# The last matrix product of a hybrid attention layer, formed by seven half products per pair of row tiles

## The chip, the cores and the metric

The kernel runs on one core of one Trainium2 chip, in one launch. The metric is device time in microseconds (us). A run takes the time of the whole execution; the span below is the part that the hardware profiler shows of the one profiled execution.

## The reference

The kernel computes a decoder layer with two attention mixers. Only its end matters here. `y_a` and `y_b` are the mixers' projections, `m_a` and `m_b` slices of an earlier projection, S = D = 1024, and all is float32.

```python
mod = c @ w_ada[l] + b_ada[l]
shift, scale, gate = jnp.split(mod, 3, axis=-1)
...
y = (jax.nn.sigmoid(m_a) * y_a + jax.nn.sigmoid(m_b) * y_b) @ w_out[l]
x = x + gate[:, None, :] * rms_norm(y, g_post[l])
```

`rms_norm(y, g)` is `y * rsqrt(mean(y*y) + eps) * g` along each row.

## The kernel before

A float32 matrix is held as two fp32r halves, high and low: ScalarE casts the high one, and a subtraction on VectorE or POOL makes the low one. A product is then three matmuls of 128x128 weights with 128x512 columns: high by high, high by low, low by high. The tile scheduler orders the instructions of each engine, waits follow from tiles and their pools (a tag with `bufs` buffers), and `chain` and `after` add an order without a wait. Products go to the eight PSUM banks in a fixed turn (`anybank`, L114).

The work around the change has three stages.

The gated stage (L954 to L1003) forms the merged `y`, transposed, in eight blocks of 128 channels, `ym`. `gated(m, "B", 1, ...)` takes for each block two halves of 512 tokens, 12 matmuls each (L956 to L958), gates from DRAM with a sigmoid on ScalarE, and one multiplication on VectorE (L985). After every second block `heads_out` loads two halves of a head pair and splits them (cast L925, subtraction L926), and for each block `w_out_block` loads 128 rows of `w_out` in two halves, casts them (L978) and subtracts on POOL (L979). `gated(m, "A", 0, ...)` then multiplies (L992) and adds (L993) for the same blocks, and the block is split: cast on ScalarE, subtraction L1003 on VectorE.

The gate sums (L1005 to L1014) make the last third of `mod`: eight loads of 512 KB into `wa`, eight VectorE instructions over 128x1024 (L1011), each with a short row that reads its sum out. `gate_rows` (L1017 to L1026) spreads `mod` times `g_post` over all partitions: a VectorE multiplication makes the operand (L1022), TensorE multiplies by ones (L1025), ScalarE copies the two halves to `ggb`.

The last product (L1063 to L1068) has eight row tiles of 128 tokens. `out_products` (L1028) makes both halves of a tile, 24 matmuls each (L1034 to L1036). `out_rows` (L1040) squares both on ScalarE (L1049), multiplies the first by its gate (L1052), makes the mean (L1053, L1055), takes the power on POOL (L1056), multiplies the second half (L1057), multiplies by the power and adds `x` (L1060), and stores (L1061). Two tiles are ahead; the gate rows stand behind them:

```python
ahead = [out_products(0), out_products(1)]
gate_rows()
for i in range(NT):
    out_rows(i, ahead.pop(0))
    if i + 2 < NT:
        ahead.append(out_products(i + 2))
```

Of the kernel before, what the change touches and what calls it, by code (L numbers as in the profile page):

```python
# [7 lines left out]
F32 = mybir.dt.float32  # L8
# [6 lines left out]
P = 128  # L15
# [52 lines left out]
def hybrid_kernel(tc, io, out):  # L68
# [843 lines left out]
    with tc.tile_pool(name="ot", bufs=1, reuse_waits="tile") as op:  # L912
        oh = [op.tile([P, S], F32R, name=f"oh{k}", tag=f"oh{k}") for k in range(8)]
        ol = [op.tile([P, S], F32R, name=f"ol{k}", tag=f"ol{k}") for k in range(8)]
        ym = {}
# [4 lines left out]
        def heads_out(k):  # L920
            for half in range(2):
# [19 lines left out]
        for n, name in enumerate(MERGE[:KEEP]):  # L941
            sg = op.tile([P, S], F32, name="sgm", tag=f"ym{7 - n}")
# [23 lines left out]
        woh, wol = [], []  # L966
        ymh, yml = [], []

        def w_out_block(k):

            a, b = [], []
            for n in range(2):
                ns = slice(n * HS, n * HS + HS)
                raw = wp.tile([P, HS], F32, name="wraw", tag="wraw", bufs=3)
                nc.sync.dma_start(raw, io["w_out"][k * P : (k + 1) * P, ns])
                a.append(main.tile([P, HS], F32R, name=f"woh{k}", tag=f"hh{k}_{n}"))
                b.append(main.tile([P, HS], F32R, name=f"wol{k}", tag=f"hl{k}_{n}"))
                nc.scalar.copy(a[n], raw)  # L978
                nc.gpsimd.tensor_tensor(b[n], raw, a[n].bitcast(F32), ALU.subtract)  # L979
            woh.append(a)  # L980
            wol.append(b)

        for m in range(8):
            ym[m] = op.tile([P, S], F32, name=f"ym{m}", tag=f"ym{m}")
            gated(m, "B", 1, lambda sl, ty, sg: nc.vector.tensor_tensor(ym[m][:, sl], ty, sg, ALU.mult))  # L985
            if m % 2:
                heads_out(m // 2)
            w_out_block(m)
        for m in range(8):

            def emit(sl, ty, sg):
                nc.vector.tensor_tensor(sg, ty, sg, ALU.mult)  # L992
                nc.vector.tensor_tensor(ym[m][:, sl], ym[m][:, sl], sg, ALU.add)  # L993
# [4 lines left out]
            ymh.append(op.tile([P, S], F32R, name=f"ymh{m}", tag=places[m][0]))  # L998
            yml.append(op.tile([P, S], F32R, name=f"yml{m}", tag=places[m][1]))
            for half in range(2):  # L1000
                sl = slice(half * HS, half * HS + HS)
                nc.scalar.copy(ymh[m][:, sl], ym[m][:, sl])
                nc.vector.tensor_tensor(yml[m][:, sl], ym[m][:, sl], ymh[m][:, sl].bitcast(F32), ALU.subtract)  # L1003

        cb2 = op.tile([P, D], F32, name="cb2", tag="ym6")  # L1005
        nc.sync.dma_start(cb2, io["c"].partition_broadcast(P))
        for k, place in enumerate(("ym7", "oh1", "ol1", "oh2", "ol2", "oh3", "ol3", "oh1")):
            blk = 16 + k
            wa = op.tile([P, D], F32, name="wa", tag=place)
            nc.sync.dma_start(wa, io["w_adaT"][blk * P : (blk + 1) * P, :])  # L1010
            nc.vector.tensor_tensor_reduce(  # L1011
                out=wa, in0=wa, in1=cb2, scale=1.0, scalar=smalls[:, 8 + blk : 9 + blk],
                op0=ALU.mult, op1=ALU.add, accum_out=mod[:, blk : blk + 1])
# [137 lines left out]
```

## Time and profile before

| | us |
|---|---|
| median of 3 runs (923.88 to 925.2) | 924.22 |
| the profiled execution | 921.23 |
| its span | 919.4 |
| busy: TensorE / VectorE / ScalarE / POOL | 905.2 / 559.2 / 507.4 / 356.2 |

The busy times are sums over the whole span; the last product takes about its last tenth. A matmul's row lasts longer than the step to the next one, because matmuls overlap. The profiled execution has its own time, and it is that time which its span belongs to.

### The profile page before, as it was taken

How to read it: one execution, taken by the hardware profiler on the slowest of the kernel's cores; microseconds unless marked ns; L12 is line 12 of the kernel's file. 1: busy time of each engine (PE TensorE's matmuls, PEld its weight loads, DVE VectorE, ACT ScalarE, POOL GpSimd, SP SyncE). 2: the span in 40 equal slices, each digit the busy share in tenths (PEclk: the TensorE clock that was granted, in tenths of full speed). 3: DMA queues.
4: the chain of work that ended last, by engine and by line, in shares of the span. 5: the costliest groups of instructions: out<-in, count | busy, mean ns of one | idle time of the engine just before them, and what ended most of it. 6: DMA issues, size and time to landing. Idle time of an engine off the chain costs nothing.

```text
span 919.4 us, 14324 instructions
## 1 busy us (share of the span) xinstructions
PE 905.2 (98%) x4584; PEld 756.9 (82%) x4584; DVE 559.2 (61%) x1522; ACT 507.4 (55%) x1151; POOL 356.2 (39%) x422
## 2 busy tenths in 40 slices
PE   9999999999999999999999999999999999999997
PEld 7888888888888878778878888887888888887885
DVE  6866754477677865784576855665564273577322
ACT  6476623467676776674666765655655465442111
POOL 0000521357566765553433764534433176200000
PEclk9999999999999999999999999999999999999999
DMA  9953441422333311212101222121211487334432
GB/s 353 319 193 98 149 148 61 138 81 90 91 106 100 105 54 44 73 36 70 63 30 36 81 64 82 37 72 35 70 57 47 167 261 232 124 103 195 138 102 81
DMA packets 63869, 100.83 MB, mean 110 GB/s; under 512 B 7473, under 2 KB 24241, under 8 KB 63794
## 3 DMA queue, kind: packets, MB, share of 16 engines
q1 hardware_dynamic: 62640, 98.69, 32.7%
q10 hardware_dynamic: 1154, 1.23, 0.5%
q8 instruction: 36, 0.59, 0.3%
q14 instruction: 39, 0.32, 0.1%
HBM read 79.97 MB, written 19.92 MB: 109 GB/s over the span
## 4 chain that ended last, share of the span: by engine, by line
PE 55%; DVE 1%; ACT 1%; issue 0%; DVEq 0%; POOLq 0%; ACTq 0%
PE b_pj L181 6%; PE b_pj L188 6%; PE b_pj L189 6%; PE b_pt L793 6%; PE b_pv L804 3%; PE b_s L740 3%; PE b_pv L801 3%; PE b_s L743 3%; PE b_s L1036 1%; PE b_s L1035 1%; PE b_s L1034 1%; PE b_s L956 1%; PE b_s L957 1%; PE b_s L958 1%; PE b_pj L957 1%; PE b_pt L1035 1%
## 5 line engine op out<-in xcount | busy, mean ns | idle before, releaser
L181 PE MATMUL b_pj<-hh,wh 128*128 128x512 f32 x528 | 210.4, 398 | 0.0
L189 PE MATMUL b_pj<-hh,wl 128*128 128x512 f32 x528 | 208.4, 395 | 0.0
L188 PE MATMUL b_pj<-hl,wh 128*128 128x512 f32 x528 | 208.2, 394 | 0.0
L158 POOL TENSOR_TENSOR wl<-wraw,wh 128x512 fp32r<-128x512 f32 x102 | 135.5, 1331 | 158.1 <-ACT wh L155 105.9
L800 DVE TENSOR_TENSOR pl<-b_pt,ph 128x512 fp32r<-128x512 f32 x178 | 120.7, 686 | 40.1 <-ACT ph L799 38.7
L799 ACT CAST ph<-b_pt 128x512 fp32r<-128x512 f32 x178 | 101.6, 583 | 58.8 <-PE b_pt L793 52.9
L189 PEld LDWEIGHTS b_pj<-hh,wl 128*128 128x128 f32 x528 | 99.4, 188 | 18.9
L181 PEld LDWEIGHTS b_pj<-hh,wh 128*128 128x128 f32 x528 | 99.4, 188 | 17.9 <-DVE sp L518 0.3
L188 PEld LDWEIGHTS b_pj<-hl,wh 128*128 128x128 f32 x528 | 99.4, 188 | 17.3
L740 PE MATMUL b_s<-kh,q 128*128 128x256 f32 (+6 forms) x264 | 86.3, 333 | 1.3 <-DVE rr L768 0.8
L764 ACT ACTIVATE ps<-ps,mins 128x256 f32<-128x256 f32 (+7 forms) x96 | 65.0, 678 | 39.6 <-DVE mins L750 38.3
L743 PE MATMUL b_s<-kl,q 128*128 128x256 f32 (+6 forms) x264 | 84.3, 323 | 0.0
L776 POOL TENSOR_SCALAR ps<-ps,rr,gates 128x128 f32<-128x128 f32 (+7 forms) x64 | 52.6, 827 | 81.1 <-DVE rr L768 71.1
L155 ACT CAST wh<-wraw 128x512 fp32r<-128x512 f32 x94 | 57.8, 617 | 43.3 <-PE b_pj L188 32.6
L764 ACT ACTIVATE pw<-pw,mins 128x256 f32<-128x256 f32 (+4 forms) x96 | 60.6, 632 | 26.9 <-DVE mins L750 25.1
L804 PE MATMUL b_pv<-pl,V 128*128 128x512 f32 x162 | 69.6, 430 | 1.6 <-DVE pl L800 1.5
L801 PE MATMUL b_pv<-ph,V 128*128 128x512 f32 x162 | 68.0, 420 | 0.7 <-DVE minc L758 0.5
L776 POOL TENSOR_SCALAR pw<-pw,rr,gates 128x640 f32<-128x640 f32 (+4 forms) x64 | 47.6, 747 | 47.7 <-DVE rr L768 44.0
L740 PEld LDWEIGHTS b_s<-kh,q 128*128 128x128 f32 x264 | 49.8, 189 | 10.1 <-DVE mins L750 2.2
L815 POOL TENSOR_TENSOR ot<-ot,zt 64x512 f32<-64x512 f32 x32 | 41.4, 1294 | 42.5 <-DVE ot L814 30.9
L743 PEld LDWEIGHTS b_s<-kl,q 128*128 128x128 f32 x264 | 49.9, 189 | 6.3
L793 PE MATMUL b_pt<-ident,ps 128*128 128x128 f32 x344 | 52.8, 273 | 0.0
(296 smaller groups left out, 1839.0 us busy)
## 6 DMA issues: line engine op xcount, KB each, us to landing
wraw<-in_w_blk SPq DMA_DIRECT2D x90, 256.0 KB, 2.8
wa<-in_w_adaT SPq DMA_DIRECT2D x24, 512.0 KB, 5.3
w1raw<-in_w SPq DMA_DIRECT2D x16, 256.0 KB, 3.0
od<-ot SPq DMA_DIRECT2D x64, 64.0 KB, 2.1
sp_MA<-sp SPq DMA_DIRECT2D x16, 256.0 KB, 2.0
wraw<-in_w_o SPq DMA_DIRECT2D x16, 256.0 KB, 3.3
wraw<-in_w_out SPq DMA_DIRECT2D x16, 256.0 KB, 3.2
t<-od SPq DMA_DIRECT2D x16, 256.0 KB, 3.8
```

Of the source, the lines that this page charges most:

```text
L158: chain("wl", nc.gpsimd.tensor_tensor(wl, raw, wh.bitcast(F32), ALU.subtract))
L181: ins = nc.tensor.matmul(t, lhsT=wh, rhs=hh[kc][half], start=(kc == 0), stop=False)
L188: nc.tensor.matmul(t, lhsT=wh, rhs=hl[kc][half], start=False, stop=False)
L189: nc.tensor.matmul(t, lhsT=wl, rhs=hh[kc][half], start=False, stop=(kc == KC - 1))
L740: ins = nc.tensor.matmul(sp[:, :n_in], lhsT=q, rhs=rh, start=True, stop=False)
L743: nc.tensor.matmul(sp[:, :n_in], lhsT=q, rhs=rl, start=False, stop=True)
L764: nc.scalar.activation(rows[r][:, :off], rows[r][:, :off], AF.Exp, scale=-1.0, bias=mins[:, n - 1, r : r + 1], accum_out=sums[:, r : r + 1])
L776: nc.gpsimd.tensor_scalar(rows[r][:, :off], rows[r][:, :off], rr[:, r : r + 1], gate, ALU.mult, ALU.mult)
L793: ins = nc.tensor.transpose(t[:kw, r * P : r * P + P], rows[r][:, off : off + kw], ident)
L799: nc.scalar.copy(ph[:kw], t[:kw])
L800: nc.vector.tensor_tensor(pl[:kw], t[:kw], ph[:kw].bitcast(F32), ALU.subtract)
L804: nc.tensor.matmul(pv, lhsT=v, rhs=pl[:kw], start=False, stop=(last and n == len(todo) - 1))
```

## The change

The product `y @ w_out` is taken as a product of 2x2 matrices: tokens in two halves (rows `p` and `p + 4` are a pair of row tiles), inner channels in two halves of four blocks, and output channels in two halves. Seven products of four blocks (12 matmuls each) and sums replace eight (Strassen's method in Winograd's form). The sums of weights, T1 to T4, are formed in the gated stage: VectorE subtracts (`sums_b` and `sums_a`), ScalarE casts and POOL subtracts (`w_set`, L978). `w_out` is loaded twice there, in whole rows. The last set, B21, is loaded behind. The sums of rows, S1 to S4, are formed per pair in the last stage (L1094). Row operands are now split there too (`split_rows`, cast L1080, subtraction L1081). Six sets stand ahead of the first product, then five ahead of each. Results are added up in SBUF by VectorE (L1171 to L1182); the row's end reads them from there. The gate sums (L1060) keep their instruction and stand behind the first sets, with three buffers; the gate rows (operand L1071, matmul L1074) stand behind the second product of the second pair. The row's end has its mean in L1130 and L1131, its power in L1132, and its multiplication and addition in L1137. Line numbers here and in the rows of the changed kernel below are the changed kernel's.

```diff
-        def w_out_block(k):
...
+        ya = [op.tile([P, 4, S], F32, name=f"ym{j}", tag=f"ym{j}") for j in range(2)]
+        def w_set(name, k, src, places):
+            a, b = places
+            W[name, k] = a, b
+            return nc.scalar.copy(a, src), nc.gpsimd.tensor_tensor(b, src, a.bitcast(F32), ALU.subtract)
+        def w_rows(k):
+            r = op.tile([P, D], F32, name="r", tag="r", bufs=2)
+            nc.sync.dma_start(r, io["w_out"][k * P : (k + 1) * P, :])
+            return r
...
+        def sums_b(m):
+            k = m // 2
+            if m % 2 == 0:
+                rows[k] = w_rows(k), w_rows(k + 4)
+                r0, r1 = rows[k]
+                w_set("B11", k, r0[:, lo_], of_h(0, k))
+                nc.vector.tensor_tensor(r0[:, hi_], r0[:, hi_], r0[:, lo_], ALU.subtract)
+                w_set("T1", k, r0[:, hi_], of_h(1, k))
+            else:
+                r0, r1 = rows.pop(k)
+                w_set("B22", k, r1[:, hi_], of_h(2, k))
+                nc.vector.tensor_tensor(r1[:, lo_], r1[:, hi_], r0[:, hi_], ALU.subtract)
+                w_set("T2", k, r1[:, lo_], of_h(3, k))
+        def sums_a(m):
...
+                nc.vector.tensor_tensor(r0[:, hi_], r1[:, hi_], r0[:, hi_], ALU.subtract)
+                w_set("T3", k, r0[:, hi_], of_heads(f"oh{k + 4}"))
+            else:
+                r0, r1 = rows.pop(k)
+                nc.vector.tensor_tensor(r1[:, lo_], r1[:, lo_], r0[:, lo_], ALU.subtract)
+                nc.vector.tensor_tensor(r1[:, lo_], r1[:, lo_], r0[:, hi_], ALU.subtract)
+                w_set("T4", k, r1[:, lo_], of_heads(f"ol{k + 4}"))
         for m in range(8):
...
             if m % 2:
                 heads_out(m // 2)
-            w_out_block(m)
+            sums_b(m)
...
             gated(m, "A", 0, emit)
-            places = [(f"oh{m + 4}", f"ol{m + 4}")] * 4 + [("ym0", "ym1"), ("ym2", "ym3"), ("ym4", "ym5"), ("oh0", "ol0")]
...
+            sums_a(m)
+        def last_set():
+            for k in range(4):
...
+                for ins, tag in zip(w_set("B21", k, raw, of_heads(f"oh{k}")), ("high", "pool")):
+                    after(ins, last[tag])
+        def gate_sums():
...
+                tag, bufs = (("r", 2), ("r", 2), ("ol2", 1))[k % 3]
+                wa = op.tile([P, D], F32, name="wa", tag=tag, bufs=bufs)
...
+        def split_rows(src, eng):
+            a = wp.tile([P, 4, P], F32R, name="wh", tag="wh", bufs=WBUFS)
+            b = wp.tile([P, 4, P], F32R, name="wl", tag="wl", bufs=WBUFS)
+            chain("high", nc.scalar.copy(a, src))
+            chain("vector" if eng is nc.vector else "pool", eng.tensor_tensor(b, src, a.bitcast(F32), ALU.subtract))
+            return a, b
+        def row_set(p, name):
+            up, down = slice(p * P, p * P + P), slice(HS + p * P, HS + p * P + P)
+            A = {"A11": ya[0][:, :, up], "A12": ya[1][:, :, up], "A21": ya[0][:, :, down], "A22": ya[1][:, :, down]}
...
+            if name == "S3":
+                form("S3", "A11", "A21", ALU.subtract)
+            elif name == "S2":
+                form("S1", "A21", "A22", ALU.add)
+                form("S2", "S1", "A11", ALU.subtract)
+            elif name == "S4":
+                form("S4", "A12", "S2", ALU.subtract)
+            return split_rows(A[name], nc.vector if p == 0 and name in ("S2", "A22", "S4") else nc.gpsimd)
+        def product(t, a, name):
+            for k in range(4):
+                bh, bl = W[name, k]
+                ins = nc.tensor.matmul(t, lhsT=a[0][:, k, :], rhs=bh, start=(k == 0), stop=False)
...
+                nc.tensor.matmul(t, lhsT=a[0][:, k, :], rhs=bl, start=False, stop=False)
+            for k in range(4):
+                nc.tensor.matmul(t, lhsT=a[1][:, k, :], rhs=W[name, k][0], start=False, stop=(k == 3))
...
+        STEPS = [("A11", "B11"), ("S3", "T3"), ("S2", "T2"), ("S1", "T1"), ("A22", "T4"), ("S4", "B22"), ("A12", "B21")]
+        todo = [(p, n) for p in range(4) for n in range(7)]
...
+        sets_to(6)
+        last_set()
+        gate_sums()
+        for step, (p, n) in enumerate(todo):
+            sets_to(step + 5)
...
+            t = anybank()
+            product(t, ready.pop((p, n)), STEPS[n][1])
+            if n == 0:
+                nc.scalar.copy(X, t)
+            elif n == 1:
+                tb = t
+            elif n == 2:
+                nc.vector.tensor_tensor(Y, X, t, ALU.add)
+                nc.vector.tensor_tensor(Z, Y, tb, ALU.add)
+            elif n == 3:
+                nc.vector.tensor_tensor(V1, Z, t, ALU.add)
+                nc.vector.tensor_tensor(Y, Y, t, ALU.add)
+            elif n == 4:
+                nc.vector.tensor_tensor(Z, Z, t, ALU.add)
+                done_rows.append((p + 4, [(1, V1, V1), (0, Z, Z)]))
+            elif n == 5:
+                nc.vector.tensor_tensor(Y, Y, t, ALU.add)
+            elif n == 6:
+                nc.vector.tensor_tensor(X, X, t, ALU.add)
+                done_rows.append((p, [(1, Y, Y), (0, X, X)]))
+            if (p, n) == (1, 1):
+                gate_rows()
+            if step > 7:
+                while done_rows:
+                    out_rows(*done_rows.pop(0))
```

The first place in the order is VectorE's, from the last gate sums to the operand of the gate rows (`mod` rows read a sum out, `t_9383` and `t_9493` are the operand's first half, `b_...` are PSUM banks). Before:

```order
L1011 ISA mod 128x1
L1011 ISA wa,mod<-wa,cb_9254,smalls 128x1024
L1011 ISA mod 128x1
L1014 TENSOR_TENSOR amod<-mod,smalls 128x8
L1022 TENSOR_TENSOR t_9383<-ident,amod 128x512
L1022 TENSOR_TENSOR t_9388<-ident,amod 128x512
L1053 TENSOR_SCALAR ss<-ss 128x1
```

With the change:

```order
L1177 TENSOR_TENSOR t_9326<-t_9326,b_pt 128x512
L1180 TENSOR_TENSOR t_9325<-t_9325,b_pj 128x512
L1060 ISA wa,mod<-wa,cb_9297,smalls 128x1024
L1060 ISA mod 128x1
L1182 TENSOR_TENSOR t_9324<-t_9324,b_s 128x512
L1130 TENSOR_SCALAR ss<-ss 128x1
L1064 TENSOR_TENSOR amod<-mod,smalls 128x8
L1130 TENSOR_SCALAR ss<-ss 128x1
L1131 TENSOR_SCALAR rs<-ss 128x1
L1071 TENSOR_TENSOR t_9493<-ident,amod 128x512
L1071 TENSOR_TENSOR t_9498<-ident,amod 128x512
```

The updates of the first pair now stand among the gate sums, and the last of them ahead of the operand.

The second place is POOL's queue, from the end of the gated stage (`wt` is a weight set's low half, `wl` a row set's; `ym_8418` and `ym_8419` are the two halves of the gated result, other `t_` names are sums of rows). Before:

```order
L158 TENSOR_TENSOR wl<-wraw,wh 128x512
L979 TENSOR_TENSOR wol_8861<-wraw,woh_8860 128x512
L979 TENSOR_TENSOR wol_8867<-wraw,woh_8866 128x512
L158 TENSOR_TENSOR wl<-wraw,wh 128x512 x8
L1056 TENSOR_TENSOR rs<-rs,neg_77 128x1 x8
```

With the change:

```order
L1081 TENSOR_TENSOR wl<-t_9249,wh 128x512
L1081 TENSOR_TENSOR wl<-t_9255,wh 128x512
L978 TENSOR_TENSOR wt<-wraw,wt 128x512 x3
L1081 TENSOR_TENSOR wl<-ym_8419,wh 128x512
L1081 TENSOR_TENSOR wl<-ym_8418,wh 128x512
L978 TENSOR_TENSOR wt<-wraw,wt 128x512
L1081 TENSOR_TENSOR wl<-t_9393,wh 128x512
L1081 TENSOR_TENSOR wl<-t_9415,wh 128x512
L1081 TENSOR_TENSOR wl<-t_9413,wh 128x512
L1081 TENSOR_TENSOR wl<-ym_8419,wh 128x512
L1081 TENSOR_TENSOR wl<-t_9473,wh 128x512
L1081 TENSOR_TENSOR wl<-ym_8419,wh 128x512
```

Where one power per row tile stood, twelve subtractions of 128x512 now stand ahead of the first power.

The third place is TensorE's, at the gate rows (`ones` times the operand). Before, the two stand together:

```order
L1035 MATMUL b_s<-wol_8867,ymh_9248 128x512
L1036 MATMUL b_s<-woh_8866,yml_9249 128x512
L1025 MATMUL b_pt<-t_9383,ones 128x512
L1025 MATMUL b_pj<-t_9388,ones 128x512
L1034 MATMUL b_s<-woh_8463,ymh_8912 128x512
L1035 MATMUL b_s<-wol_8464,ymh_8912 128x512
```

With the change, the first, and after 17 matmuls more the second:

```order
L1112 MATMUL b_pt<-wt,wh 128x512
L1114 MATMUL b_pt<-wt,wl 128x512 x4
L1074 MATMUL b_s<-t_9493,ones 128x512
L1109 MATMUL b_s<-hhw_8516,wh 128x512
L1112 MATMUL b_s<-hlw_8517,wh 128x512
L1109 MATMUL b_s<-hhw_8628,wh 128x512
```

```order
L1112 MATMUL b_pt<-hlw_8570,wh 128x512
L1109 MATMUL b_pt<-hhw_8681,wh 128x512
L1074 MATMUL b_pj<-t_9498,ones 128x512
L1112 MATMUL b_pt<-hlw_8682,wh 128x512
L1109 MATMUL b_pt<-hhw_8793,wh 128x512
```

Both still stand among the products, but products of the third and fourth step now part them.

## Rows read from the trace of the kernel before

**Rows 1.** The page's busy us, share of the span and instructions, by engine.

```profile
PE 905.2 (98%) x4584; PEld 756.9 (82%) x4584; DVE 559.2 (61%) x1522; ACT 507.4 (55%) x1151; POOL 356.2 (39%) x422
```

**Rows 2.** Stretch, us, busy of PE, PEld, DVE, ACT, POOL; clock, DMA share, GB/s.

```profile
740.00:760.00 20.00, 20.00 (x90) 16.57 (x89) 15.45 (x17) 11.96 (x20) 14.20 (x11) 1.00 0.78 249
...
800.00:822.00 22.00, 22.00 (x99) 18.23 (x98) 15.79 (x26) 9.26 (x17) 0.00 (x0) 1.00 0.32 102
822.00:850.00 28.00, 28.00 (x122) 22.48 (x121) 21.52 (x39) 6.92 (x15) 1.11 (x2) 1.00 0.45 177
850.00:880.00 30.00, 30.00 (x134) 24.86 (x133) 9.52 (x19) 3.44 (x10) 1.09 (x2) 1.00 0.43 138
```

**Rows 3.** Timeline of PE in the last product: start us, us, line, matmul.

```profile
823.72 0.39 PE L958 MATMUL b_pv<-oh,wl 128*128 128x512 f32 x1
823.94 0.39 PE L1034 MATMUL b_pt<-woh,ymh 128*128 128x512 f32 x1
...
845.70 1.02 PE L1025 MATMUL b_pt<-t,ones 128*128 128x512 f32 x2
...
847.65 0.40 PE L1035 MATMUL b_s<-wol,ymh 128*128 128x512 f32 x1
...
912.52 0.39 PE L1036 MATMUL b_s<-woh,yml 128*128 128x512 f32 x1
```

**Rows 4.** Timeline of all engines behind the last matmul, [idle before <-releaser].

```profile
912.95 0.60 ACT L1049 ACTIVATE t<-b_s 128x512 f32<-128x512 f32 x1 [4.75 <-PE b_s L1036]
...
913.80 0.68 DVE L1057 TENSOR_TENSOR t<-b_s,ggb 128x512 f32<-128x512 f32 x1
914.33 0.55 POOL L1056 TENSOR_TENSOR rs<-rs,neg 128x1 f32<-128x1 f32 x1 [10.63 <-DVE rs L1055]
914.91 1.41 DVE L1060 SCALAR_TENSOR_TENSOR t<-t,rs,xr 128x512 f32<-128x512 f32 x2 [0.43 <-POOL rs L1056]
```

**Rows 5.** Timeline of VectorE: two products in a row, two gate sums.

```profile
759.62 0.68 DVE L985 TENSOR_TENSOR ym<-b_s,t 128x512 f32<-128x512 f32 x1
760.21 0.68 DVE L985 TENSOR_TENSOR ym<-b_pv,t 128x512 f32<-128x512 f32 x1
...
833.32 1.28 DVE L1011 CUSTOM_DVE_ANT_0 wa<-wa,cb,smalls 128x1024 f32<-128x1024 f32 x1
...
834.52 1.28 DVE L1011 CUSTOM_DVE_ANT_0 wa<-wa,cb,smalls 128x1024 f32<-128x1024 f32 x1
```

**Rows 6.** Timelines of VectorE and then POOL, 734 to 748 us.

```profile
734.75 0.69 DVE L926 TENSOR_TENSOR ol<-t,oh 128x512 fp32r<-128x512 f32 x1 [2.96 <-ACT oh L925]
...
739.55 1.06 DVE L926 TENSOR_TENSOR ol<-t,oh 128x512 fp32r<-128x512 f32 x1 [0.65 <-ACT oh L925]
741.12 1.27 DVE L926 TENSOR_TENSOR ol<-t,oh 128x512 fp32r<-128x512 f32 x1 [0.51 <-ACT oh L925]
743.91 2.94 DVE L926 TENSOR_TENSOR ol<-t,oh 128x512 fp32r<-128x512 f32 x2 [1.52 <-ACT oh L925]
746.77 0.68 DVE L985 TENSOR_TENSOR ym<-b_pt,sgm 128x512 f32<-128x512 f32 x1
747.37 1.18 DVE L926 TENSOR_TENSOR ol<-t,oh 128x512 fp32r<-128x512 f32 x1
...
735.31 1.29 POOL L979 TENSOR_TENSOR wol<-wraw,woh 128x512 fp32r<-128x512 f32 x1 [4.08 <-ACT woh L978]
...
740.54 1.30 POOL L979 TENSOR_TENSOR wol<-wraw,woh 128x512 fp32r<-128x512 f32 x1 [0.48 <-ACT woh L978]
...
744.65 1.65 POOL L158 TENSOR_TENSOR wl<-wraw,wh 128x512 fp32r<-128x512 f32 x1
746.34 1.66 POOL L979 TENSOR_TENSOR wol<-wraw,woh 128x512 fp32r<-128x512 f32 x1
```

**Rows 7.** L1011 alone, the gate sums: ns min/median/max, first and last start.

```profile
L1011 DVE CUSTOM_DVE_ANT_0 wa<-wa,cb,smalls x8: 1280/1285/1286, 831.5 to 841.3; 128x1024 f32<-128x1024 f32 x8
```

**Rows 8.** The tile of the gate sums' loads, 800 to 850 us.

```profile
DMA to landing us min/median/max: 3.4/6.5/9.4
```

More of the change, by code (lines that the diff above doesn't have):

```diff
@@ L1000, in hybrid_kernel @@
[L1000 to L1013, printed above, removed]
@@ new lines, in gate_sums @@
+        def gate_sums():
+            cb2 = op.tile([P, D], F32, name="cb2", tag="ol1")
+            nc.sync.dma_start(cb2, io["c"].partition_broadcast(P))
+            for k in range(8):
+                blk = 16 + k
+                tag, bufs = (("r", 2), ("r", 2), ("ol2", 1))[k % 3]
+                wa = op.tile([P, D], F32, name="wa", tag=tag, bufs=bufs)
+                nc.sync.dma_start(wa, io["w_adaT"][blk * P : (blk + 1) * P, :])
+                ins = nc.vector.tensor_tensor_reduce(
+                    out=wa, in0=wa, in1=cb2, scale=1.0, scalar=smalls[:, 8 + blk : 9 + blk],
+                    op0=ALU.mult, op1=ALU.add, accum_out=mod[:, blk : blk + 1])
+                after(ins, last["vector"])
+            nc.vector.tensor_tensor(amod, mod[:, 16:24], g_post, ALU.mult)
@@ L1026, in gate_rows @@
                 nc.scalar.copy(ggb[:, n * HS : n * HS + HS], t)
-        def out_products(i):
-            sl = slice(i * P, i * P + P)
-            ts = []
-            for n in range(2):
-                t = anybank()
-                for k in range(8):
-                    nc.tensor.matmul(t, lhsT=ymh[k][:, sl], rhs=woh[k][n], start=(k == 0), stop=False)
-                    nc.tensor.matmul(t, lhsT=ymh[k][:, sl], rhs=wol[k][n], start=False, stop=False)
-                    nc.tensor.matmul(t, lhsT=yml[k][:, sl], rhs=woh[k][n], start=False, stop=(k == 7))
-                ts.append(t)
-            return ts
@@ L1059, in out_rows @@
+            for j, (n, t, y) in enumerate(parts):
                 ns = slice(n * HS, n * HS + HS)
-                nc.vector.scalar_tensor_tensor(yg[n], yg[n], rs[:, 0:1], xs[n], ALU.mult, ALU.add)
-                nc.sync.dma_start(out[sl, ns], yg[n])
-        ahead = [out_products(0), out_products(1)]
-        gate_rows()
-        for i in range(NT):
-            out_rows(i, ahead.pop(0))
-            if i + 2 < NT:
-                ahead.append(out_products(i + 2))
+                nc.vector.scalar_tensor_tensor(y, y, rs[:, 0:1], xs[j], ALU.mult, ALU.add)
+                nc.sync.dma_start(out[sl, ns], y)
@@ new lines, in hybrid_kernel, with sets_to @@
+        STEPS = [("A11", "B11"), ("S3", "T3"), ("S2", "T2"), ("S1", "T1"), ("A22", "T4"), ("S4", "B22"), ("A12", "B21")]
+        todo = [(p, n) for p in range(4) for n in range(7)]
+        ready = {}
+        done_rows = []
+        at_set = [0]
+        def sets_to(k):
+            while at_set[0] < min(k, len(todo)):
+                p, n = todo[at_set[0]]
+                ready[p, n] = row_set(p, STEPS[n][0])
+                at_set[0] += 1
+        sets_to(6)
+        last_set()
+        gate_sums()
@@ new lines, in hybrid_kernel @@
+        for step, (p, n) in enumerate(todo):
+            sets_to(step + 5)
+            if n == 0:
+                if p % 2 == 0:
+                    X, Y, Z = (tmp("t1", 3) for _ in range(3))
+                    V1 = op.tile([P, 2, HS], F32, name="cx", tag="ol3")[:, 0, :]
+                else:
+                    XY, ZV = (op.tile([P, 2, HS], F32, name="cx", tag=tag) for tag in ("ol1", "ol2"))
+                    X, Y, Z, V1 = XY[:, 0, :], XY[:, 1, :], ZV[:, 0, :], ZV[:, 1, :]
+            t = anybank()
+            product(t, ready.pop((p, n)), STEPS[n][1])
+            if n == 0:
+                nc.scalar.copy(X, t)
[20 more added lines that the diff above has]
+                    out_rows(*done_rows.pop(0))
```

80 lines of the change are left out of this document (43 added, 37 removed).

## The prediction

> **What bounds the kernel now.** I read the page's busy shares first, then the table by stretch, then the timeline of the last product on TensorE, then VectorE and POOL in the stage ahead of it. TensorE is busy for 98% of the span [rows 1], and the table shows that it is the only one: in every stretch of these rows PE is busy in every microsecond at full clock. VectorE falls from 21.5 of 28 us at the start of the last product to 9.5 of the next 30, and POOL, which had 14.2 of 20 us in the gated stage, to 1.1 of 30 [rows 2]. So the last product is a pure TensorE stage. The timeline gives its size [rows 3]: the last gated matmul (L958) starts at 823.72, the last matmul of the output (L1036) at 912.52. Consecutive matmuls start 0.227 us apart (96 of them from 823.94 to 845.70). 384 of them (8 row tiles, 2 halves, 8 blocks, 3 terms) are 87.1 us, and the gate rows (L1025) take the 1.9 us from 845.70 until the stream is regular again at 847.65. From the start of the last matmul to the end of the span are 6.9 us [rows 4].
>
> **What goes.** Seven half products per pair of row tiles are 4 x 7 x 12 = 336 matmuls: 48 fewer, 48 x 0.227 = 10.9 us on the bounding engine, every one on the path. If nothing else mattered, the last matmul would start at 912.5 - 10.9 = 901.6. The tail behind it gains one VectorE operation, the sum X (L1182), which comes ahead of the square: 0.7 us, as L1057 in [rows 4]. That gives a span of 901.6 + 0.7 + 6.9 = 909.2, 10.2 less.
>
> **What comes on VectorE and POOL.** The split of the product's rows leaves the gated stage (16 casts, 16 subtractions L1003) and comes back as 28 casts and 28 subtractions (25 on POOL, 3 on VectorE), with 16 sums, in the product stage. Seven updates per pair add the products up. The row's end now reads SBUF, not PSUM in its square and in its multiplication by the gate. So I counted VectorE's rows in the order of the change, from the last gated product to the end.
>
> First stretch, from 824.1 (823.72 plus 0.39) to the operand of the gate rows (L1071): 19 sums, updates, multiplications and subtractions that start 0.60 us apart at best, 11.5 us; 8 gate sums (L1060 of the change) at 1.20, 9.6 us [rows 5]; small ones 0.7 and L1071 itself 0.7. Together 22.5 us, so 846.6. TensorE comes to the first gate row 108 matmuls after 823.94, at 848.4. Undisturbed, it would not wait at all.
>
> But POOL, idle in this stage before, now has 12 subtractions queued in that stretch (the second place in the order), 1.29 us each alone [rows 6]. The price of a meeting is in the gated stage [rows 6]: a VectorE subtraction with both inputs in SBUF takes 0.69 alone, and 1.06, 1.27 and 1.18 us when POOL is in the middle of an operation; the last two end 0.55 us after POOL's do (742.39 after 741.84, 748.55 after 748.00). Two in a row take 2.94, the second behind a whole POOL operation. POOL's own stretch from 1.29 to 1.65 and 1.66. At 746.77 an operation that reads PSUM runs beside POOL in 0.68. So the two engines take turns, and only operations with one input in PSUM escape. In the first stretch 11 sums and the 8 gate sums have both inputs in SBUF. No row shows a gate sum beside POOL: in its rows (1280 to 1286 ns) POOL is idle [rows 7]. The ends for it are 0 and the 1.3 us of a whole POOL operation; I take turns as for the others, since it reads two full SBUF tensors as L926 does. The page "SBUF — State Buffer" of the Trainium skill, section "SBUF: two separate sides", speaks against this change here: the port pair that the two engines share is an exclusive lock, held for the whole instruction by whichever starts first, for a VectorE operation with two SBUF inputs against a POOL operation that reads SBUF. L926 agrees [rows 6]; by the page the gate sums would wait as well, which is the upper end, while by the rows alone the lower end stays open.
>
> VectorE always has its next operation ready here, so it comes when POOL has just begun. I take 11 of the 12 to meet one, at 1.1 us: 12.1 us. The operand is ready at 846.6 + 12.1 = 858.7, and TensorE stands still for about 10 us: **nearly all that the seven products save is given back at the gate rows.** Bounds of this term: 0 and 12 x 1.29 = 15.5. The loads of the gate sums don't decide: three buffers instead of eight delay them, but a load lands in 3.4 us at best, 6.5 in the median [rows 8], and VectorE needs about that for three gate sums and what stands between them.
>
> Second stretch, from there to the end, again by VectorE's order: 45 sums, updates and multiplications at 0.60 (27.2 us with the odd 0.69), 16 row updates L1137 at 0.66 (10.6; the two of before's L1060 take 1.41 with their ends [rows 4]), 13 small ones (1.8), the second L1071 (0.7): 40.3 us. POOL still has 14 subtractions; 24 of these VectorE operations read two SBUF tensors and so do the 16 row updates; I take 11 meetings at 1.1, 12.1 us (ends 0 and 14 x 1.29 = 18). VectorE also waits in order: 2.5 us for the second gate row, which TensorE now issues 18 matmuls after the first (the third place in the order), and in each of the last four rows about 1.6 us for its own square and power (912.95 to 914.91 [rows 4], less what a multiplication covers): 8.9 us. Together 61.3, so VectorE ends at 858.7 + 61.3 = 920.0, and the stores end 3.1 us after that, as before (from 916.3 to 919.4 [rows 4]): **a span of 923.1, 3.7 us longer.** TensorE is through at about 913 and no longer decides the end.
>
> **Costed at nothing.** In the gated stage 20 sums take the place of the 16 subtractions on VectorE, POOL gets 8 subtractions more, and 16 loads of 512 KB and 4 of 256 stand for 16 of 256. The cover: products are taken up in 2.7 us steps (12 x 0.227) and eight banks allow a lag of several; the DMA share [rows 2] is 0.78 at its highest there and 0.32 at the end. If that cover fails, late next are the heads' loads at the stage's start, which now stand in SP's queue behind loads that wait for POOL; there a lag of one step, about 3 us, would be lost.
>
> **The sum.** The profiled execution is 921.2 us for its span of 919.4, so 921.2 + 3.7 = 924.9. The median of the runs shown is 924.2, 3.0 above it; on that scale 924.2 + 3.7 = 927.9.
>
> **The rivals.** *TensorE stays the bound* (faster). If meetings are rare, because POOL's queue waits for casts while VectorE is in PSUM, the gate rows are ready before 848.4 and the span is 909.2: 914.0 on the median's scale; with some meetings, up to 918.5. For it: undisturbed, VectorE is ready 1.8 us ahead of TensorE, and before the change TensorE waited for nothing. Against it: POOL's queue is full just there, and VectorE's is never empty. It decides from the point where meetings ahead of the gate rows cost under 1.8 us.
>
> *The gate sums don't wait.* Then only 5 of the 11 meetings remain in the first stretch, 6 x 1.1 = 6.6 us less; the operand is ready at 852.1, and the span is 916.5: 2.9 us less than before, 921.3. For it: they are another kind of instruction than any that is seen to wait [rows 6]. Against it: two SBUF inputs.
>
> *More is late than the gate rows.* A start of the gated stage that waits for the heads, at about 3 us, and meetings at their full 1.29 in both stretches (22 x 0.19 = 4.2 us more) give 935. For it: POOL and VectorE already share that stage at 14.2 and 15.5 of 20 us [rows 2]. Against it: TensorE is busy for 20.00 of 20 us there.
>
> **How the numbers follow.** 0.2% are 1.85 us, about what a measurement of this kernel can tell from no change. My forecast has 0.52, TensorE bound 0.24, gate sums free 0.14, more late 0.10. The likeliest case's own range is 925 to 932, with meetings at 0.95 to 1.29 us. The range over all, 916 to 932, leaves out half of the fast rival and most of the late one. Slower: the late rival and all but 0.08 of the forecast, 0.54; faster: the fast rival and 0.08 of the gate sums', 0.32; same: the rest, 0.14.
>
> **What would show it.** Right: the gate sums (L1060 of the change) at 1.8 to 2.5 us instead of 1.28; PE idle some 10 us just ahead of L1074, released by VectorE's L1071; row updates L1137 well over 0.75; VectorE's busy time near full from 824 to the end; several us of VectorE work after the last matmul. Wrong: those at 1.28 (second rival), or no idle PE before L1074 and a last matmul near 902 (first). A wait at PE ahead of 800 would be the third.

## The result and the profile after

The change makes the kernel slower: 934.12 us against 922.78 of the kernel before on the same chip (medians of six runs each), a ratio of 1.0115 with a 95% interval of 1.0098 to 1.0131. The profiled execution took 932.37 us for a span of 930.6. The forecast was 927.9 (916 to 932) and slower: the sign is right, the size too small, and 934.12 lies above the range. 11.3 us were lost, 3.7 were forecast.

The page's busy times answer to [rows 1]: TensorE has its 48 matmuls less, VectorE 61 us more, POOL 65 us more.

```profile
PE 900.4 (97%) x4536; PEld 752.1 (81%) x4536; DVE 620.2 (67%) x1573; ACT 521.2 (56%) x1179; POOL 420.8 (45%) x459
```

The table by stretch (columns as in [rows 2]) shows where it went. TensorE is no longer busy throughout: 5.5 us are missing in 822 to 850 and 9.8 in 850 to 880, both at a lower granted clock, and VectorE is nearly full there and up to 900. Ahead of them, from 780 to 800, VectorE is half idle while TensorE is full.

```profile
780.00:800.00 20.00, 20.00 (x90) 16.57 (x89) 10.42 (x15) 7.35 (x13) 8.22 (x6) 1.00 0.50 170
...
822.00:850.00 28.00, 22.48 (x91) 18.11 (x90) 26.98 (x33) 10.70 (x19) 15.70 (x9) 0.88 0.48 158
850.00:880.00 30.00, 20.19 (x75) 14.92 (x74) 29.49 (x42) 10.25 (x22) 19.25 (x13) 0.83 0.25 85
880.00:900.00 20.00, 20.00 (x89) 16.54 (x89) 19.18 (x27) 7.47 (x16) 11.89 (x10) 1.00 0.55 171
```

What TensorE waited for from 680 us to the end (us in total, times, longest) names three waits. The line at the top is for the gate rows' operand, the later wait in time; the one below it, the earlier in time and called the first wait from here on, is for the cast of the first sum of rows, S3; the third is for a weight set.

```profile
PE b_s L1074 <- DVE t L1071: 9.3, 1, 9.3
PE b_s L1109 <- ACT wh L1080: 5.5, 1, 5.5
...
PE b_s L1112 <- POOL wt L978: 0.5, 1, 0.5
```

TensorE's timeline, to be read against [rows 3], has the first matmul of the product, the two waits, and matmuls behind them, 0.43 us apart where 0.227 is the rule:

```profile
824.30 0.39 PE L1109 MATMUL b_pt<-hhw,wh 128*128 128x512 f32 x1
...
832.70 0.79 PE L1109 MATMUL b_s<-wt,wh 128*128 128x512 f32 x1 [5.52 <-ACT wh L1080]
833.29 0.63 PE L1112 MATMUL b_s<-wt,wh 128*128 128x512 f32 x1
833.72 0.63 PE L1109 MATMUL b_s<-wt,wh 128*128 128x512 f32 x1
...
837.52 0.39 PE L1109 MATMUL b_pj<-hhw,wh 128*128 128x512 f32 x1
...
866.83 2.08 PE L1074 MATMUL b_s<-t,ones 128*128 128x512 f32 x2 [9.26 <-DVE t L1071]
...
869.13 0.63 PE L1112 MATMUL b_s<-hlw,wh 128*128 128x512 f32 x1
869.56 0.63 PE L1109 MATMUL b_s<-hhw,wh 128*128 128x512 f32 x1
...
921.54 1.07 PE L1114 MATMUL b_pj<-wt,wl 128*128 128x512 f32 x4
```

From the first matmul to the start of the last (922.22, the fourth of that last group) the product takes 97.9 us; before it took 88.6 (823.94 to 912.52). The 9.3 us are the 10.9 saved, 15.3 of waits, 4.3 of matmuls at the slow pace (twelve took 4.82 us from 832.70 where 2.72 are due, and about as much was lost behind 866.83), and 0.6 of small things. The tail behind it is 8.4 us instead of 6.9 [rows 4].

Why the operands were late stands in VectorE's timeline. In the gated stage it stood still four times for the two rows of w_out (tile r) from which the sets T3 and T4 are formed (L1018), 23.1 us in all; it began the last gated multiplication (L1036) at 832.94 and ended the stage (L1037) at 834.7; then came the gate sums (L1060), the first three beside POOL, the last two alone; the operand L1071 was begun at 866.09.

```profile
780.15 0.69 DVE L1018 TENSOR_TENSOR r<-r 128x512 f32<-128x512 f32 x1 [7.34 <-DMA r<-in_w_out]
...
795.25 1.58 DVE L1018 TENSOR_TENSOR r<-r 128x512 f32<-128x512 f32 x1 [8.52 <-DMA r<-in_w_out]
...
807.90 0.69 DVE L1018 TENSOR_TENSOR r<-r 128x512 f32<-128x512 f32 x1 [4.00 <-DMA r<-in_w_out]
...
818.41 0.69 DVE L1018 TENSOR_TENSOR r<-r 128x512 f32<-128x512 f32 x1 [3.27 <-DMA r<-in_w_out]
...
829.05 0.69 DVE L1094 TENSOR_TENSOR t<-ym 128x512 f32<-128x512 f32 x1
...
832.94 0.68 DVE L1036 TENSOR_TENSOR t<-b_pv,t 128x512 f32<-128x512 f32 x1
833.66 1.05 DVE L1037 TENSOR_TENSOR ym<-ym,t 128x512 f32<-128x512 f32 x1
...
843.19 2.31 DVE L1060 CUSTOM_DVE_ANT_0 wa<-wa,cb,smalls 128x1024 f32<-128x1024 f32 x1
...
863.56 1.27 DVE L1060 CUSTOM_DVE_ANT_0 wa<-wa,cb,smalls 128x1024 f32<-128x1024 f32 x1
...
866.09 1.29 DVE L1071 TENSOR_TENSOR t<-ident,amod 128x512 f32<-128x512 f32 x2
```

What SP's queue waited for between 740 and 840 us shows why those loads came late: a load of r (L982) is issued when VectorE and POOL are through with the buffer, and a load of a gate (L934) when a gated addition has freed its buffer.

```profile
SPq L934 <- DVE ym L1037: 17.7, 10, 5.4
...
SPq L982 <- POOL wt L978: 5.5, 3, 4.3
...
SPq L982 <- DVE r L1023: 1.3, 1, 1.3
```

The first wait has one link more. S3 (L1094) was formed by 829.74, but its cast (L1080) began at 832.04: on ScalarE it stood behind the last sigmoid of a gate (L935), which waited for such a load. No run parts these 2.3 us from the rest.

```profile
831.51 0.63 ACT L935 ACTIVATE t<-t 128x512 f32<-128x512 f32 x1 [0.62 <-DMA t<-sp_MA]
832.04 0.60 ACT L1080 CAST wh<-t 128x512 fp32r<-128x512 f32 x1
```

POOL's timeline beside the first gate sums: its subtractions, 1.29 us alone [rows 6], take 2.25 here.

```profile
844.38 4.50 POOL L1081 TENSOR_TENSOR wl<-ym,wh 128x512 fp32r<-128x512 f32 x2
```

The kernel before was not punctual there either. The last gated multiplication on its VectorE (L992) began at 827.38 and the last addition (L993) ended at 829.49, 5.5 us behind the first matmul of the product. No one waited for it: these are tokens 512 to 1023, which the fifth row tile reads first. In the change each pair of row tiles needs both halves of the tokens.

```profile
827.38 0.69 DVE L992 TENSOR_TENSOR t<-b_pv,t 128x512 f32<-128x512 f32 x1
...
828.81 0.68 DVE L993 TENSOR_TENSOR ym<-ym,t 128x512 f32<-128x512 f32 x1
```

The chain that ended last (start, us, engine and line) runs over loads of r and of a gate, with POOL and VectorE between them, then over VectorE up to the gate rows, and over TensorE behind them:

```profile
790.32 4.80 DMA r<-in_w_out
...
814.02 4.27 DMA r<-in_w_out
...
825.06 4.47 DMA t<-sp_MA
...
863.63 1.20 DVE wa L1060
866.83 2.08 PE b_s L1074 x2
871.81 0.93 PE b_s L1114 x4
```

### The profile page after: what moved, and what is told of

The parts are those of the page before. It is cut to its first block, busy times and chain, and to the rows that moved or that the text cites. A ratio compares the mean times of both kernels' runs of the same rounds, so it can differ in the third digit from the quotient of the medians.

```text
span 930.6 us, 14465 instructions
## 1 busy us (share of the span) xinstructions
PE 900.4 (97%) x4536; PEld 752.1 (81%) x4536; DVE 620.2 (67%) x1573; ACT 521.2 (56%) x1179; POOL 420.8 (45%) x459
## 4 chain that ended last, share of the span: by engine, by line
PE 46%; DVE 5%; issue 3%; DMA 2%; ACT 1%; POOL 1%; DVEq 0%; POOLq 0%; SPq 0%; ACTq 0%
PE b_pj L181 6%; PE b_pj L188 5%; PE b_pj L189 5%; PE b_pt L793 5%; PE b_pv L804 3%; PE b_s L740 3%; PE b_s L743 3%; PE b_pv L801 3%; DMA r<-in_w_out 1%; DVE wa L1060 1%; DVE t L1094 1%; PE b_s L1109 1%; PE b_s L1112 1%; PE b_s L1114 1%; PE b_s L957 1%
## 5 line engine op out<-in xcount | busy, mean ns | idle before, releaser
L181 PE MATMUL b_pj<-hh,wh 128*128 128x512 f32 x528 | 210.5, 399 | 0.0
L181 PEld LDWEIGHTS b_pj<-hh,wh 128*128 128x128 f32 x528 | 99.5, 188 | 17.9 <-DVE sp L518 0.3
```

The lines of the kernel that those rows point to most:

```text
L181: ins = nc.tensor.matmul(t, lhsT=wh, rhs=hh[kc][half], start=(kc == 0), stop=False)
```

## The experiments

My theory, A: two separate things are late, each with a wait of its own. In the gated stage, VectorE waits for the loads of T3 and T4 and so brings the first row sum late; in the product stage, the gate sums and POOL's turns bring the gate rows late. Rivals: the turns with POOL alone (B), or VectorE's mere amount of work, wherever it stands (C).

The profiled executions came to the product's first matmul anywhere between 823.94 and 828.02 us with almost the same program ahead of it, so the profiles are compared by the length of the product on TensorE, from its first matmul to the start of its last. (f2 to f4 have other work at the start and come there later.) This scatter arises in the first 54 us: the first matmul of L181 (an early projection) starts at 50.19 before and at 50.49 in the change, and at 53.25 to 53.45 in e1 and e4. The medians of the kernel before differ between the rows too, so times are compared by the ratios.

| kernel | median us (before beside it) | ratio, 95% | product, us | waits in it over 1 us |
|---|---|---|---|---|
| before | | | 88.6 | none |
| the change | 934.12 (922.78) | 1.0115 [1.0098, 1.0131] | 97.9 | 5.5, 9.3 |
| e1_no_late_sums | 927.16 (921.7) | 1.003 [1.001, 1.005] | 89.9 | 9.2 |
| e2_split_vector | 935.32 (921.7) | 1.0128 [1.0086, 1.0169] | 99.8 | 5.2, 1.3, 10.0 |
| e3_gate_later | 934.3 (921.7) | 1.0122 [1.0099, 1.0146] | 90.5 | 3.1, 2.8, 1.5 |
| e4_loads_ahead | 927.43 (921.7) | 1.0053 [1.0034, 1.0072] | 90.9 | 9.3 |
| e5_no_gate_sums | 921.5 (924.31) | 0.9974 [0.9957, 0.9992] | 83.9 | 4.2 |
| e6_no_pool | 922.51 (924.31) | 0.9988 [0.9968, 1.0008] | 85.2 | 5.4 |
| f1_sums_early | 928.3 (924.31) | 1.0044 [1.0023, 1.0066] | 91.6 | 5.8, 3.4 |
| f2_sums_at_start | 928.23 (924.35) | 1.0056 [1.0039, 1.0074] | 84.0 | 3.1 |
| f3_start_ahead | 922.15 (924.35) | 0.9983 [0.9967, 0.9998] | 77.7 | none |
| f4_start_behind | 920.83 (924.18) | 0.9971 [0.9954, 0.9987] | 77.7 | none |

**e1_no_late_sums.** The sets T3 and T4 are not formed in the second half of the gated stage; their products read T1 and T2.

```diff
             gated(m, "A", 0, emit)
-            sums_a(m)
+        for k in range(4):
+            W["T3", k], W["T4", k] = W["T1", k], W["T2", k]
```

> Leaves out the sums T3 and T4 of the weights (eight loads of 512 KB, twelve VectorE subtractions, eight casts and eight POOL subtractions of the second half of the gated stage); the products use T1 and T2 in their place. Theory A, late loads: VectorE waits in order 8.5, 4.0 and 3.3 us for loads of w_out there, so that its last gated addition starts at 833.7 where it was 828.8 before. Without them it starts at 829 or earlier, the 5.5 us wait of TensorE for the first sum of rows goes, and the operand of the gate rows comes about 5 us earlier than 866.1; the time falls by about that, to 929. TensorE's wait at the gate rows stays at 9 us or grows, since TensorE comes earlier too. Theory B, only the turns of VectorE and POOL in the product stage count: the operand stays at 866, and the time at 933 to 935.

Measured: the first wait is gone, the second is not. VectorE's last gated addition starts at 827.98, 1.0 us behind the product's first matmul (826.99), where it was 9.4 behind; the operand of the gate rows comes at 860.06. The only wait over 1 us:

```profile
PE b_s L1075 <- DVE t L1072: 9.2, 1, 9.2
```

So the first wait hangs on the sums T3 and T4 and their loads, by which VectorE leaves the gated stage late. It disappears without any change to the turns with POOL in the product stage, which B can't explain.

**e4_loads_ahead.** All sets are formed; the loads of T3 and T4 are issued up to two steps ahead, two of them into buffers that are free by then (e4 has lines of its own: L1082 is L1074 of the change).

```diff
+        def ahead_a(k):
+            if k == 1:
+                rows[k] = w_rows(k, "oh7", 1), w_rows(k + 4, "ol7", 1)
...
+        PLAN = {0: [(ahead_a, 1), (t3, 0)], 1: [(t4, 0)], 2: [(ahead_a, 2), (t3, 1)], 3: [(t4, 1)],
+                4: [(t3, 2), (t4, 2)], 5: [(ahead_a, 3)], 7: [(t3, 3), (t4, 3)]}
```

> Same work as the change, but the loads for T3 and T4 stand ahead: the first two behind the first half of the gated stage, the next two in places of the heads that are free by then, so that only the last two wait for a buffer. Theory A: VectorE's waits for these loads (8.5, 4.0, 3.3 us) go or shrink below 3 in sum, its last gated addition starts at 829 to 830, and the operand of the gate rows comes 4 to 5 us earlier; 929 to 930. Theory B: no gain over 1 us.

Measured: 927.43, by the ratios not clearly apart from leaving the sums out. VectorE still waits for r in three places, 13.4 us in place of 23.1, but its last gated addition starts 3.0 us behind the product's first matmul (830.73 after 827.69), and the first wait of TensorE is gone:

```profile
PE b_s L1082 <- DVE t L1079: 9.3, 1, 9.3
PE b_s L1120 <- POOL wt L978: 1.0, 1, 1.0
```

The lateness that TensorE felt was thus the loads' and not the sums' work: with all of the work kept, about 6 us come back (ratio 1.0053 after 1.0115), and about 8 where the sums are left out (1.003).

**e5_no_gate_sums** and **e6_no_pool.** The first leaves out the eight gate sums, the second POOL's subtractions in the last stage (the product then takes the rounded high parts in place of the low ones; of e6 the row sets are shown, the last set of weights goes the same way).

```diff
...
-                ins = nc.vector.tensor_tensor_reduce(
-                    out=wa, in0=wa, in1=cb2, scale=1.0, scalar=smalls[:, 8 + blk : 9 + blk],
-                    op0=ALU.mult, op1=ALU.add, accum_out=mod[:, blk : blk + 1])
-                after(ins, last["vector"])
-            nc.vector.tensor_tensor(amod, mod[:, 16:24], g_post, ALU.mult)
+            nc.vector.tensor_tensor(amod, mod[:, 0:8], g_post, ALU.mult)
```

```diff
             chain("high", nc.scalar.copy(a, src))
+            if eng is nc.gpsimd:
+                return a, a
```

> The change with the eight gate sums and their loads left out (the gate rows use another third of the sums). Theory: they hold VectorE for 15.0 us (eight at 1.27 to 2.31) between the last gated addition and the operand of the gate rows, which would then be ready at about 851, before TensorE comes there (856.5 to 857.4). Its 9.3 us wait and the 2 us at the lower clock go, the 5.5 us wait for the first sum of rows stays: 922 to 924. If the gate sums' 15 us are not what TensorE waits for, or VectorE's work behind them sets the end in any case, less than 5 us are gained.

> The change without POOL's subtractions in the last stage: the low halves of 25 row sets and of the last set of weights are left out, the products use the high half in their place, so that no other engine takes the work. Theory of turns: 10.4 us of VectorE's time ahead of the operand go, the gate sums are at 1.28 us, the operand is ready at about 856, when TensorE comes there, and the time is 922 to 925. Row updates L1137 go from 1.3 to 0.75 us. Rival, the turns are covered by other waits: the operand stays later than 862 and the time above 929.

Measured: both take the second wait away and leave the first, 4.2 and 5.4 us:

```profile
PE b_s L1098 <- ACT wh L1069: 4.2, 1, 4.2
```

```profile
PE b_s L1112 <- ACT wh L1080: 5.4, 1, 5.4
```

Either part alone fits into the time that VectorE has ahead of the gate rows; the two together do not. So the second wait comes from these two together, as A has it, and the first from neither of them. C would explain these two runs as well, since both take time from VectorE; f2 and f3, which keep all of the work, are the test for that.

**e2_split_vector.** VectorE makes all 28 subtractions of the row sets itself; POOL keeps those of the weight sets.

```diff
...
-            return split_rows(A[name], nc.vector if p == 0 and name in ("S2", "A22", "S4") else nc.gpsimd)
+            return split_rows(A[name], nc.vector)
```

> All 28 subtractions of the row sets on VectorE, none on POOL. Theory of turns: each POOL subtraction costs VectorE about 1.05 us where it meets it, more than the 0.6 us that it takes on VectorE itself. In the stretch from 834.7 to the gate rows' operand 10.4 us of turns go and some 6.5 us of subtractions come; the gate sums return to 1.28 us from 1.9; the operand is some 3.5 us earlier, and the time 930 to 931. Rival, turns cost VectorE nothing that it did not have to spare: the operand is 6.5 us later, and the time 940.

Measured: 935.32, no gain, which I had not expected. Six gate sums now take their 1.27 us, the other two still meet the weight sets' subtractions on POOL, but from the end of the last gated addition to the operand VectorE needs 30.9 us against 31.4 of the change:

```profile
838.34 0.69 DVE L1037 TENSOR_TENSOR ym<-ym,t 128x512 f32<-128x512 f32 x1
...
846.94 2.32 DVE L1059 CUSTOM_DVE_ANT_0 wa<-wa,cb,smalls 128x1024 f32<-128x1024 f32 x1
...
865.86 1.27 DVE L1059 CUSTOM_DVE_ANT_0 wa<-wa,cb,smalls 128x1024 f32<-128x1024 f32 x1
...
869.93 1.28 DVE L1070 TENSOR_TENSOR t<-ident,amod 128x512 f32<-128x512 f32 x2
```

Ahead of the operand VectorE got ten subtractions more, 0.60 us apart, 6.0 us; the turns, what rows take beyond their time alone, fell from 10.4 to 4.2 us. The expectation had let all of the turns go.

**e3_gate_later.** The gate rows stand four products later, and the row ends follow.

```diff
-            if (p, n) == (1, 1):
+            if (p, n) == (1, 5):
                 gate_rows()
-            if step > 7:
+            if step > 11:
```

> The gate rows behind the sixth product of the second pair in place of the second, and the first row ends four steps later. Theory: TensorE reaches them 48 matmuls, 10.9 us, later, so its 9.3 us wait there and the 2 us at the lower clock behind it go. VectorE then has the row ends later; from its busy time behind 834.7, some 84 us, it ends no earlier than 919, so that of the 11 us some 6 to 8 are left: 926 to 928. If VectorE alone set the end as forecast, the time would not move by more than 2 us: 932 to 936. If it only moves TensorE's wait to another place, that wait is seen there.

Measured: 934.3, no gain either. The wait for the gate rows falls from 9.3 to 4.3 us in two parts (the first wait was 3.1 in this profile), and the product is 7.4 us shorter, yet VectorE has its row ends still to do: its last operation starts 9.1 us behind TensorE's last matmul (4.1 in the change).

```profile
917.80 1.07 PE L1114 MATMUL b_pj<-wt,wl 128*128 128x512 f32 x4
```

```profile
927.55 1.42 DVE L1137 SCALAR_TENSOR_TENSOR cx<-cx,rs,xr 128x512 f32<-128x512 f32 x2 [0.44 <-POOL rs L1132]
```

From the end of the last gated addition to its own end VectorE takes 92.9 us here (836.08 to 928.97) and 93.0 in the change (834.71 to 927.72). As far as the end goes, C is right: shifting the point at which TensorE asks gains nothing while VectorE's own work from there to the end stays the same.

**f1_sums_early.** e4, and the gate sums in halves among VectorE's work in the second half of the gated stage.

```diff
+            if m < 7:
+                gate_sum(m)
+            if m == 6:
+                gate_sum(7)
...
         last_set()
-        gate_sums()
```

> The kernel with the loads ahead, and with the gate sums moved into the second half of the gated stage, one per block, in halves of 512 columns, in buffers that are free there. All work is kept. Theory: VectorE has time between the gated blocks (10 to 13 of 20 us busy), the operand of the gate rows is ready long before TensorE comes to it, no wait of TensorE over 2 us is left, and the last matmul starts some 75 us behind the first of the last product, at about 902: span 911 to 914, time 914 to 917, faster than both kernels. Rival: VectorE, with the row ends and their turns, then sets the end; its work behind the gated stage was 84 us with 15 us of gate sums, so 70 us from 831, and with waits for its own squares up to 80: span 914 to 918, time 917 to 921. If the gate sums make the gated stage late instead, TensorE waits before 825.

Measured: 928.3, missed. The gate rows wait no longer, but VectorE leaves the gated stage late again (its half sums begin between 800.32 and 837.92, the last gated addition at 839.98), and TensorE stands 5.8 and 3.4 us for the first row sums. The stretch shows it: VectorE full, the clock down.

```profile
822.00:850.00 28.00, 18.74 (x65) 14.51 (x64) 27.52 (x46) 10.07 (x18) 8.56 (x6) 0.76 0.43 140
```

VectorE's half-idle time in that stage was not free to use: it is spent waiting in order for loads of r, one of them for 7.34 us, and the half sums stood behind these waits. The DMA share was higher too, 0.82 between 780 and 800 (0.50 in the change); what that adds no run shows.

**f2_sums_at_start** and **f3_start_ahead.** The gate sums stand at 110 to 160 us, in the projections at the kernel's start, in f2 with the loads of T3 and T4 as in the change, in f3 as in e4. Nothing is left out.

```diff
+        plan = {1: (0,), 2: (1,), 3: (2,), 4: (3, 4), 5: (5,), 6: (6, 7)}
+        for n, _ in enumerate(zs):
+            if n in plan:
+                gate_sums(plan[n])
```

> The change with its gate sums moved to 110 to 160 us, where TensorE is busy without a gap, VectorE at some 40% and the DMA queues at 16 to 40%; their buffers are free there. All work is kept. Theory: as without the gate sums, 920 to 923: TensorE's 9.3 us wait at the gate rows goes, the wait of about 4 us for the first sum of rows stays. If the gate sums only cost where they stand because VectorE is late, and cost as much at the start, 930 or more.

> The gate sums at 110 to 160 us and the loads for T3 and T4 ahead: both causes taken away, all work kept. Theory: both waits of TensorE go (5.5 and 9.3 us) with the time at the lower clock behind them; the gains of the two, 12.6 and 6.7 us, add up or nearly so, as the first wait is what is left without the gate sums: last matmul at about 903, time 913 to 917, faster than the kernel before by 5 to 9 us. Rival: VectorE and POOL in the last stage then set the end, as they did with the gate rows later: no better than 920.

Measured: f3's product takes 77.7 us without a wait, which is the 88.6 of before less the 10.9 of the 48 matmuls; f2's takes 84.0, with the first wait left. With all of the work kept, f3 thus has neither wait: they hang on where the work and its loads stand, and not on VectorE's amount of work (C). But both are slower than expected, since the start lost most of what the end gained, in f3 6.8 us: from the first matmul of L181 to the product TensorE takes 780.6 us, and 773.8 before. In f3 VectorE waited for the gate sums' loads, with the product for the gate's projection (L518) queued behind it, and TensorE waited for that. VectorE, then TensorE:

```profile
122.31 1.28 DVE L659 CUSTOM_DVE_ANT_0 wa<-wa,cb,smalls 128x1024 f32<-128x1024 f32 x1 [2.77 <-DMA wa<-in_w_adaT]
...
127.08 1.28 DVE L659 CUSTOM_DVE_ANT_0 wa<-wa,cb,smalls 128x1024 f32<-128x1024 f32 x1 [2.53 <-DMA wa<-in_w_adaT]
```

```profile
134.03 0.80 PE L181 MATMUL b_pj<-hh,wh 128*128 128x512 f32 x1 [3.33 <-DVE sp L518]
```

**f4_start_behind.** As f3, with each sum one half block behind its load and directly behind that half block's L518.

```diff
-        plan = {1: (0,), 2: (1,), 3: (2,), 4: (3, 4), 5: (5,), 6: (6, 7)}
+        plan = {3: (0,), 4: (1,), 5: (2,), 6: (3, 4), 7: (5,), 8: (6, 7)}
...
+            gate_sums(in_wait)
+            in_wait = gate_loads(plan[n]) if n in plan else []
```

> The change with the loads of the third and fourth sets a step ahead and the gate's sums at the kernel's start, as in f3_start_ahead, but each sum now stands on VectorE one half block of the gate's projection behind its load, directly after that half block's own product, so that VectorE is not to wait for a load there. Nothing is left out. In f3_start_ahead TensorE waited 3.3 us for VectorE at 130 to 134 us behind two such waits of VectorE (2.8 and 2.5 us), and then ran some six matmuls at 0.43 us apart: 5.3 us in all. Theory (the whole loss at the start hangs on VectorE waiting for two loads): that stretch shows no wait of TensorE, everything behind it starts some 5 us earlier, and the time is 916 to 918 us against 922.15 of f3_start_ahead. Rival 1 (the loads crowd SyncE's queue, and the blocks' own loads come late whatever VectorE does): TensorE waits elsewhere between 130 and 180 us, and the time stays at 921 to 923. Rival 2 (starting the last stages earlier brings VectorE's lag back there): the first row sums or the row ends hold TensorE again, 919 to 921.

Measured: 920.83, faster than before by 0.29% (interval 0.13 to 0.46), the lowest ratio here, though not clear of f3's 0.9983 or of e5's. The wait at 134 us is gone, and the product again has none:

```profile
828.77 0.39 PE L1127 MATMUL b_pt<-hhw,wh 128*128 128x512 f32 x1
...
905.79 1.07 PE L1132 MATMUL b_pj<-wt,wl 128*128 128x512 f32 x4
```

The median falls short of the 916 to 918 expected (the profiled execution took 917.78). In the profile the product is 10.9 us shorter than before's and the tail 2.6 longer (916.0 less 906.47, against 6.9), but the product starts at 828.77 and not at 823.94. TensorE's waits up to 822 us add up to 9.3 us there, 7.0 before; the longest single one that is new is 1.2 us for VectorE's L598 at 148 us. So 2.3 of the 4.8 us are seen as waits; the rest stays open. Against f3 little came back: from the first matmul of L181 to the product are 778.5 us here, 2.1 less than in f3. The other 3.3 us by which the product starts earlier than in f3 (834.17) lie ahead of that matmul, in the scatter of the first 54 us. So the wait at 134 us did hang on VectorE's waits for the loads, but the whole loss at the start did not. The time is that of rival 2, whose sign, a wait in the last product, is not there.

## Why the forecast was right in its sign and too small

By the forecast's own steps, in the profile's time:

| step | forecast | measured |
|---|---|---|
| 48 matmuls less | -10.9 | -10.9 (f3, f4: 77.7 for 88.6) |
| VectorE begins the first stretch (L1036, the last gated product) | 824.1 | 832.9 |
| first stretch, to the operand's use | 34.6 | 33.9 (to 866.8) |
| second stretch, to VectorE's end | 61.3 | 60.9 (to 927.7) |
| the stores behind it | 3.1 | 2.9 |
| span | 923.1 | 930.6 |

**The step that failed is "First stretch, from 824.1 (823.72 plus 0.39)".** I let VectorE begin the last stage when TensorE ends the gated one. It began 8.8 us later, and that is more than the whole miss of 7.5 us (8.8 - 0.7 - 0.4 - 0.2). Some 3.3 of the 8.8 stood in the trace that I had: VectorE's last gated multiplication began at 827.38. I read TensorE's rows at that border, and not VectorE's. The other 5.5 are a failure of **"Costed at nothing"**: the cover that I named, a lag of several steps that the banks allow, did hold for TensorE (20.00 of 20 us in each stretch from 720 to 800, 22.00 of 22 up to 822), but VectorE came out of the stage with the lag. I had looked for a collision at the stage's start, in SP's queue; it came in its second half, in a pair of buffers for r whose refill had to wait for VectorE and POOL. e1 and e4 show it: without the sums, or with their loads ahead, the first wait is gone and some 8 or 6 us with it.

**The turns with POOL were right.** Twelve operations of the first stretch took longer than alone, 10.7 us in all, where 11 meetings and 12.1 us were forecast. Six of the eight gate sums took 1.72 to 2.31 us (forecast 1.8 to 2.5), the two that met no POOL operation 1.27, as in [rows 7]. So the second rival, that they don't wait, is out; e2 brings six of them back to 1.27 by taking POOL away. The rule of the Trainium skill (page "SBUF — State Buffer", section "SBUF: two separate sides"), an exclusive lock held for the whole instruction, agrees with the trace in that both engines wait. By it a gate sum and a subtraction in turn would take 1.28 + 1.29 = 2.57 us, an estimate from [rows 5] and [rows 6]. Measured are 2.23 a pair (843.19 to 849.89 for three), so the two rows of a pair overlap by some 0.3 us.

**The wait at the gate rows, about 10 us forecast and 9.3 measured, is right by luck, by two errors that cancel.** The operand came at 866.8 and not at 858.7. TensorE, held by the wait that I had not seen and by the slow matmuls behind it, was there at 857.6 and not at 848.4.

**Who sets the end was nearly a tie.** I had TensorE through at 913 and VectorE at 920. TensorE was through at 922.6, VectorE at 927.7, and the chain names TensorE from the gate rows on. VectorE's length of 61.3 was sized well, and e3 shows that it stands close behind: when TensorE is through earlier, VectorE keeps the end.

**The rivals.** TensorE as the bound (914 to 918.5) is what the saved matmuls are worth when the operands are there in time: with both repairs the product took its full 10.9 us less, and f4, 920.83, came nearest in time. The late rival's 935 is near the measured time and its heading is right, since more than the gate rows was late; but its mechanism, a wait of TensorE at the gated stage's start, did not happen.

## What to carry to other kernels

When a change fills an engine that was idle, read where that engine stands at the border of the stage, by its own last rows, and not where the bounding engine stands: a lag that costs nothing before is the starting point of everything that is added. A saving on the bounding engine is worth its full sum only when the side work that feeds it is placed where its engine has time and its loads are there a step ahead, and the place that it moves to has its own price (here 4.8 to 6.8 of the 10.9 us); removing one late input leaves the wait for the other in full, and moving the consumer back gains nothing when the feeder also sets the end. A sum that waits for a load should stand behind work that the load's delay can hide, since in an engine that works in order everything behind it waits as well; in f4 that took the wait away and gave back some 2 us.

## What the runs showed of the hardware

A wait of TensorE cost more than its length. Behind the first wait of the change (5.5 us) seven steps in a row from one matmul to the next were 0.43 us, behind the second (9.3 us) four, in place of 0.227, that is at 1.2 GHz in place of 2.4, and the granted clock was 0.88 and 0.83 in these stretches: 2.1 and 2.2 us beside the waits. In f3, behind the wait of 3.3 us at 134 us, five steps were at the slow pace too.

A row update that reads two SBUF tensors (L1137) took between 0.74 and 1.78 us in the change: 0.74 at 881.00, where POOL was idle, and 1.78 at 903.97, beside a subtraction on POOL that began at 903.71.
